# Attention inside a hybrid decoder layer: the scores of a group of heads in one burst, its outputs in one block, its transposes two stages later

## The chip, the cores and the metric

The kernel runs on one core of a Trainium2 chip. The metric is the device time of one execution in microseconds (us); lower is better. Three runs of the kernel before took 1525.62, 1527.35 and 1528.2 us, a median of 1527.35 us.

## What is computed

One decoder layer in float32: 256 tokens, model width 2048. After a norm and one wide input projection, a recurrent branch and an attention branch run side by side, are gated, added and projected, and an MLP of width 8192 follows. The change is in the attention branch alone. It has 32 query heads and 4 key heads of 64 elements; eight query heads share one key head, and these eight are called a group here. Attention goes by blocks of 128 tokens. A query block sees its own block and the one before it, within a window of 128, and each head has a learned sink that takes part in the softmax:

```python
scores = jnp.einsum('bnqhgd,bnkhd->bnhgqk', qb, kk).astype(jnp.float32)   # qb is scaled
scores = jnp.where(valid, scores, NEG_INF)
m = jnp.maximum(jnp.max(scores, axis=-1, keepdims=True), sink)
p = jnp.exp(scores - m)
denom = jnp.sum(p, axis=-1, keepdims=True) + jnp.exp(sink - m)
out = jnp.einsum('bnhgqk,bnkhd->bnqhgd', (p / denom).astype(v.dtype), vv)
```

With 256 tokens there are two query blocks: `tb` 0 sees 128 keys, `tb` 1 sees 256.

## The kernel before

**The stream.** All weights pass through one stream (class `Stream`). SyncE loads halves of 128x1024 float32 (`wraw`, four buffers), ScalarE rounds each to a high part (`whi`, line 94), VectorE subtracts to get the low part (`wlo`, line 95). There are six buffers each of `whi` and `wlo`, and the parts are made six halves ahead, so the cast of half j+6 waits for TensorE to have finished half j. TensorE multiplies each half three ways (high by high, low by high, high by low). In `b_pass512` a half is 12 matmuls of 512 columns (lines 271, 273, 275; outputs `g` and `q`); in `a_pair` it is 8 matmuls of 512 and 8 of 256 columns (lines 253 and 256; output `ps`). Eight halves make one pass. For every group of heads one `g` pass (gates) and one `q` pass (queries) follow each other.

**The attention of a group** is the generator `attention(g, banks)`. It is created after the `q` pass of its group and put on the list `waiting`. The passes that follow call `pump()`, which runs the first generator of the list up to its next `yield`: the `g` pass of the next group pumps after each half, its `q` pass after every second half, `a_pair` after each half. Groups 0, 1 and 2 are so laid into the `g` and `q` passes of groups 1, 2 and 3, and group 3 into the first `a_pair` passes of the recurrent branch. The pumping sets where a step is recorded. A scheduler then orders the instructions of each engine within what the data allow, except for those that `pin` (`tc.keep_in_program_order`) holds in the order of the program. Each engine then works off its instructions strictly in that order.

**Steps of one group.** (1) Rope on the queries, four transposes each for two token blocks into `pq` (line 518), a copy to `qT`. (2) Scores: for a head pair, the two heads lie on partitions 0 to 63 and 64 to 127 of `qT`, so each score matmul uses 64 rows of the array; the two of a pair go to two PSUM banks `sc` (line 540). (3) VectorE scales and masks each bank into `s` (line 547) and takes the row maxima (line 549), three small operations (lines 553 to 555) fold in the sink, ScalarE takes one exponential per head with its row sum (line 560; the sink's is line 556), VectorE adds, inverts (lines 562, 563) and multiplies (line 565). (4) Transposes of the probabilities: four heads of 128x128 into a bank `pt` (line 574), ScalarE copies it to `s` or `pT` (line 576). (5) Outputs: 64-column matmuls with the values `v_sb` into `po` (line 582), the two heads of a pair on the two halves of the columns; ScalarE and VectorE split `po` into `yatt` (lines 586, 587).

For `tb` 0 these are 8 score matmuls of 128 columns, 8 transposes and 2 output matmuls of 512 columns; for `tb` 1, 8 score matmuls of 256 columns, 16 transposes and 4 output matmuls. The profile counts each float32 score and output matmul twice (two passes), each transpose once. Before, `tb` 0 goes through steps 2 to 5 and then `tb` 1 does. All of `pq`, `sc`, `pt` and `po` come from one pool of two PSUM banks (`psm`); another pool of two (`psb`) holds the outputs of the `q` pass, and two pairs of banks (`psa`, handed out by `pair`) hold the outputs of the `g` and `a_pair` passes.

Of the kernel before, what the change touches and what calls it, by code (L numbers as in the profile page):

```python
# [18 lines left out]
F32 = mybir.dt.float32  # L19
# [147 lines left out]
def layer(tc, x, g_pre, pos_t, pos_row, inv_freq, vecs, sinks, gains, w_kv, w_q, w_xy, w_rg, w_g, w_rp, w_ap, w_out,  # L167
# [341 lines left out]
    def attention(g, banks):  # L509
# [11 lines left out]
        for tb in range(TB):  # L521
            yield
            nk = 1 + tb
            w = P * nk
            per = 512 // w
            room = flat(unit("s", F32)).rearrange("p (n c) -> p n c", c=512)
            if tb:
                room_p = flat(unit("pT", F32)).rearrange("p (n c) -> p n c", c=512)
            else:
                room_p = room[:, 2:4, :]  # L530
            stat = pa.tile([P, 4, 8], F32, tag="stat", bufs=3, name="stat")
            sk = sink[:, 8 * g : 8 * g + 8]
            tiles = []
            for j in range(4 // per):
                both = [bank(psm, "sc") for par in range(2)]
                for i in range(per):
                    h = j * per + i
                    for par in range(2):
                        r0 = par * HD
                        mm(both[par][:, i * w : i * w + w], qT[r0 : r0 + HD, h, tb * P : tb * P + P],  # L540
                           kT[r0 : r0 + HD, g, 0:w], start=True, stop=True)
                for par in range(2):
                    ps = both[par]
                    at = par * 4 + j * per
                    s3 = room[:, at // per, :].rearrange("p (h k) -> p h k", h=per)
                    mk = (mask1 if tb else mask0).unsqueeze(1).to_broadcast([P, per, w])
                    nc.vector.scalar_tensor_tensor(s3, ps.rearrange("p (h k) -> p h k", h=per), HD ** -0.5, mk,
                                                   ALU.mult, ALU.add)
                    nc.vector.tensor_reduce(stat[:, 0, at : at + per], s3, AX.X, ALU.max)
                    tiles.append((s3, at))  # L550
                if tb:
                    yield
# [4 lines left out]
            for s3, at in tiles:  # L557
                for i in range(per):
                    c = slice(at + i, at + i + 1)
                    nc.scalar.activation(s3[:, i, :], s3[:, i, :], AF.Exp, bias=stat[:, 1, c],  # L560
                                         accum_out=stat[:, 3, c])
            nc.vector.tensor_tensor(stat[:, 2, :], stat[:, 2, :], stat[:, 3, :], ALU.add)
            nc.vector.reciprocal(stat[:, 2, :], stat[:, 2, :])
            for s3, at in tiles:
                nc.vector.tensor_tensor(s3, s3, stat[:, 2, at : at + per].unsqueeze(2).to_broadcast([P, per, w]),
                                        ALU.mult)
            yield
            pT = {}
            for par in range(2):
                for kb in range(nk):  # L570
                    ps = bank(psm, "pt")
                    for h in range(4):
                        s3, at = tiles[h // per * 2 + par]
                        nc.tensor.transpose(ps[:, h * P : h * P + P], s3[:, h % per, kb * P : kb * P + P], ident)
                    t = room_p[:, par * nk + kb, :]
                    nc.scalar.copy(t, ps)
                    pT[par, kb] = t
            yield
            po = bank(psm, "po")
            for kb in range(nk):  # L580
                for par in range(2):
                    mm(po[par * HD : par * HD + HD, :], v_sb[:, kb, g * HD : g * HD + HD], pT[par, kb],
                       start=kb == 0, stop=kb == nk - 1)
# [676 lines left out]
```

## Time and profile before

| | |
|---|---|
| runs | 1525.62, 1527.35, 1528.2 us (median 1527.35) |
| profiled execution, its own time | 1523.52 us |
| span of its instructions | 1521.7 us |
| mean granted TensorE clock | 0.999 of full |
| TensorE (PE) busy | 1506.0 us, 99% of the span |
| VectorE (DVE) busy | 1105.1 us, 73% |
| ScalarE (ACT) busy | 831.3 us, 55% |

All times in the text are us from the start of the span. In a timeline a row gives the start, the length, the engine, the line and operation, the tiles (written, then read), the shape, how many instructions were merged in it, and in brackets the idle time of the engine ahead of it with what ended it. Matmuls are pipelined: the start of one to the start of the next is what one costs, and the lengths overlap.

### The profile page before, as it was taken

How to read it: one execution, taken by the hardware profiler on the slowest of the kernel's cores; microseconds unless marked ns; L12 is line 12 of the kernel's file. 1: busy time of each engine (PE TensorE's matmuls, PEld its weight loads, DVE VectorE, ACT ScalarE, POOL GpSimd, SP SyncE). 2: the span in 40 equal slices, each digit the busy share in tenths (PEclk: the TensorE clock that was granted, in tenths of full speed). 3: DMA queues.
4: the chain of work that ended last, by engine and by line, in shares of the span. 5: the costliest groups of instructions: out<-in, count | busy, mean ns of one | idle time of the engine just before them, and what ended most of it. 6: DMA issues, size and time to landing. Idle time of an engine off the chain costs nothing.

```text
span 1521.7 us, 20058 instructions
## 1 busy us (share of the span) xinstructions
PE 1506.0 (99%) x7600; PEld 1263.7 (83%) x7600; DVE 1105.1 (73%) x1377; ACT 831.3 (55%) x1143; POOL 5.5 (0%) x11
## 2 busy tenths in 40 slices
PE   9999999999999999999999999999999999999997
PEld 7877778788888888888888888888888888888886
DVE  6666666857759867555667866688886766788897
ACT  6545645746556757444355655555444555555553
POOL 0000000000000000000000000000000000000001
PEclk9999999999999999999999999999999999999999
DMA  6645445354655565555764755556667655566665
GB/s 252 221 153 166 138 142 168 128 188 161 215 184 189 169 219 177 197 195 191 263 225 131 274 198 189 187 182 216 213 202 237 205 187 192 188 230 200 216 221 178
DMA packets 82896, 296.20 MB, mean 195 GB/s; under 512 B 9712, under 2 KB 9968, under 8 KB 81648
## 3 DMA queue, kind: packets, MB, share of 16 engines
q1 hardware_dynamic: 79056, 284.43, 56.4%
q10 hardware_dynamic: 3744, 10.50, 1.9%
q8 instruction: 59, 0.97, 0.3%
q14 instruction: 37, 0.30, 0.1%
HBM read 288.60 MB, written 6.29 MB: 194 GB/s over the span
## 4 chain that ended last, share of the span: by engine, by line
PE 90%; DVE 4%; ACT 2%; DMA 2%; issue 2%; SPq 0%; DVEq 0%; ACTq 0%
PE ps L253 21%; PE ps L256 11%; PE dQ L1036 8%; PE s L1036 4%; PE pp L273 4%; PE pp L275 4%; PE pp L271 4%; PE dP L1036 4%; PE g L271 4%; PE g L275 4%; PE g L273 4%; PE dCs L1036 3%; PE q L271 2%; PE q L273 2%; PE q L275 2%
## 5 line engine op out<-in xcount | busy, mean ns | idle before, releaser
L95 DVE TENSOR_TENSOR wlo<-wraw,whi 128x1024 fp32r<-128x1024 f32 x523 | 634.4, 1222 | 306.2 <-ACT whi L94 304.6
L94 ACT CAST whi<-wraw 128x1024 fp32r<-128x1024 f32 x523 | 544.3, 1051 | 567.4 <-PE ps L253 139.2
L253 PE MATMUL ps<-h2T,whi 128*128 128x512 f32 x960 | 240.5, 393 | 0.0
L253 PEld LDWEIGHTS ps<-h2T,whi 128*128 128x128 f32 x960 | 172.9, 189 | 30.7
L256 PEld LDWEIGHTS ps<-h2T,wlo 128*128 128x128 f32 x960 | 131.0, 191 | 9.3
L256 PE MATMUL ps<-h2T,wlo 128*128 128x256 f32 x960 | 133.9, 283 | 0.0
L253 PE MATMUL ps<-hT,whi 128*128 128x512 f32 x512 | 130.0, 394 | 0.0
L1036 PE MATMUL dQ<-whi,uT 128*128 128x512 f32 x288 | 107.0, 389 | 0.0
L253 PEld LDWEIGHTS ps<-hT,whi 128*128 128x128 f32 x512 | 91.8, 189 | 16.8 <-issue 0.7
L271 PE MATMUL g<-whi,hT 128*128 128x512 f32 x256 | 101.7, 397 | 0.0
L273 PE MATMUL g<-wlo,hT 128*128 128x512 f32 x256 | 100.4, 392 | 0.1
L275 PE MATMUL g<-whi,hT 128*128 128x512 f32 x256 | 100.2, 391 | 0.0
L256 PEld LDWEIGHTS ps<-hT,wlo 128*128 128x128 f32 x512 | 69.8, 191 | 6.3 <-issue 1.5
L256 PE MATMUL ps<-hT,wlo 128*128 128x256 f32 x512 | 71.9, 283 | 0.0
L1036 PEld LDWEIGHTS dQ<-whi,uT 128*128 128x128 f32 x288 | 54.1, 188 | 11.2
L271 PEld LDWEIGHTS g<-whi,hT 128*128 128x128 f32 x256 | 48.1, 188 | 10.9 <-issue 1.3
L275 PEld LDWEIGHTS g<-whi,hT 128*128 128x128 f32 x256 | 48.1, 188 | 10.6 <-issue 0.7
L273 PEld LDWEIGHTS g<-wlo,hT 128*128 128x128 f32 x256 | 48.2, 188 | 9.7 <-DVE wlo L95 0.5
L1036 PE MATMUL dQ<-wlo,uT 128*128 128x512 f32 x144 | 56.1, 389 | 0.0
L130 DVE TENSOR_TENSOR tlo<-t,thi 128x1536 fp32r<-128x1536 f32 x28 | 49.2, 1757 | 6.8 <-ACT thi L129 6.8
L1036 PE MATMUL dP<-whi,uT 128*128 128x512 f32 x144 | 54.1, 389 | 0.0
L1036 PE MATMUL dCs<-whi,uT 128*128 128x512 f32 x144 | 54.1, 389 | 0.0
(280 smaller groups left out, 2477.4 us busy)
## 6 DMA issues: line engine op xcount, KB each, us to landing
wraw<-in_w_up SPq DMA_DIRECT2D x128, 512.0 KB, 4.7
wraw<-in_w_dn SPq DMA_DIRECT2D x128, 512.0 KB, 4.6
wraw<-in_w_g SPq DMA_DIRECT2D x64, 512.0 KB, 4.8
wraw<-in_w_xy SPq DMA_DIRECT2D x64, 512.0 KB, 4.6
wraw<-in_w_q SPq DMA_DIRECT2D x32, 512.0 KB, 3.7
wraw<-in_w_ap SPq DMA_DIRECT2D x32, 512.0 KB, 4.7
wraw<-in_w_rp SPq DMA_DIRECT2D x32, 512.0 KB, 4.4
wraw<-in_w_out SPq DMA_DIRECT2D x32, 512.0 KB, 5.2
```

The source lines that it names most:

```text
L94: self.pin(self.nc.scalar.copy(hi, src))
L95: self.pin(self.nc.vector.tensor_tensor(lo, src, hi.bitcast(F32), ALU.subtract))
L130: v.tensor_tensor(lo, t, hi.bitcast(F32), ALU.subtract)
L253: mm(both, hi[:, k * P : k * P + P], a.rearrange("p a b -> p (a b)"), start=half == 0 and k == 0, stop=False)
L256: mm(ps[:, f, 1, :], lo[:, k * P : k * P + P], a[:, 0, :], start=False, stop=half == 1 and k == 7)
L271: mm(banks[tb][n], a[:, 0, t], hi[:, n * 512 : n * 512 + 512], start=first, stop=False)
L273: mm(banks[tb][n], a[:, 0, t], lo[:, n * 512 : n * 512 + 512], start=False, stop=False)
L275: mm(banks[tb][n], a[:, 1, t], hi[:, n * 512 : n * 512 + 512], start=False, stop=last)
L1036: mm(b, a[x], w[y], start=not begun and i == 0, stop=tail and i == 2)
```

## The change

The generator is cut in functions, and the order of its steps changes:

- **Scores.** Both token blocks are computed at one place, at the third `yield`: the banks of `tb` 0 from `psm`, half of those of `tb` 1 from `psb`, and the other half from a pair of `psa`, so that six banks are in use. The matmuls are pinned in program order, which alternates the two heads of a pair. In the last group the second half of `tb` 1 comes one stage later, from `psb` again.
- **Softmax** of `tb` 0 follows at once, that of `tb` 1 a stage later.
- **Transposes** of `tb` 0 two stages after the scores, those of `tb` 1 two stages after that.
- **Outputs** of both blocks at the end, pinned.

No operation is added or removed: there are the same matmuls, transposes, copies and vector operations.

```diff
-        for tb in range(TB):
-            yield
-            nk = 1 + tb
...
-            for j in range(4 // per):
-                both = [bank(psm, "sc") for par in range(2)]
...
-                        mm(both[par][:, i * w : i * w + w], qT[r0 : r0 + HD, h, tb * P : tb * P + P],
-                           kT[r0 : r0 + HD, g, 0:w], start=True, stop=True)
...
-                if tb:
-                    yield
+        def scores(tb, j, both):
...
+            for i in range(per):
+                h = j * per + i
                 for par in range(2):
+                    r0 = par * HD
+                    pin(mm(both[par][:, i * w : i * w + w], qT[r0 : r0 + HD, h, tb * P : tb * P + P],
+                           kT[r0 : r0 + HD, g, 0:w], start=True, stop=True))
+            for par in range(2):
...
+                nc.vector.scalar_tensor_tensor(s3, both[par].rearrange("p (h k) -> p h k", h=per), HD ** -0.5, mk,
+                                               ALU.mult, ALU.add)
+                nc.vector.tensor_reduce(stats[tb][:, 0, at : at + per], s3, AX.X, ALU.max)
...
+        def softmax(tb):
...
+        def turn_probs(tb):
...
+        last_group = g == NKV - 1
+        scores(0, 0, [bank(psm, "sc") for par in range(2)])
+        scores(1, 0, [bank(psb, "sc") for par in range(2)])
+        if not last_group:
+            scores(1, 1, two_banks("sc"))
+        softmax(0)
+        yield
+        if last_group:
+            scores(1, 1, [bank(psb, "sc") for par in range(2)])
+        softmax(1)
+        yield
+        turn_probs(0)
+        yield
+        yield
+        turn_probs(1)
+        yield
+        for tb in range(TB):
             po = bank(psm, "po")
-            for kb in range(nk):
+            for kb in range(1 + tb):
                 for par in range(2):
-                    mm(po[par * HD : par * HD + HD, :], v_sb[:, kb, g * HD : g * HD + HD], pT[par, kb],
-                       start=kb == 0, stop=kb == nk - 1)
+                    pin(mm(po[par * HD : par * HD + HD, :], v_sb[:, kb, g * HD : g * HD + HD], pT[tb, par, kb],
+                           start=kb == 0, stop=kb == tb))
```

The functions hold the lines that stood in the loop, in the same order within each.

The order of instructions shows what the scheduler makes of it. First TensorE in group 1, around the end of the `g` pass, as it stands before. `pt` are the transposes, `po` the outputs, `sc` the scores, `s` the probabilities; `g` and `q` are matmuls of the stream.

```order
L574 MATMUL pt<-ident,s 128x128 x8
L273 MATMUL g<-wlo_1306,hT_136 128x512
L275 MATMUL g<-whi_1305,hT_136 128x512
L582 MATMUL po<-s,v_sb 64x512 x2
L540 MATMUL sc<-kT,qT_1266 128x256 x2
L271 MATMUL g<-whi_1305,hT_136 128x512
L273 MATMUL g<-wlo_1306,hT_136 128x512
L275 MATMUL g<-whi_1305,hT_136 128x512
L540 MATMUL sc<-kT,qT_1266 128x256 x2
```

The scores of `tb` 1 stand in three places (a block of four follows), two of them with both matmuls of one bank next to each other, and the outputs of `tb` 0 stand alone. With the change, the same group has its scores together some 50 rows earlier, and its outputs together at the end:

```order
L275 MATMUL g<-whi_1209,hT_134 128x512
L537 MATMUL sc<-kT,qT_1265 128x128 x8
L537 MATMUL sc<-kT,qT_1265 128x256 x8
L271 MATMUL g<-whi_1227,hT_135 128x512
...
L271 MATMUL q_1529<-whi_1329,hT_133 128x512
L581 MATMUL pt<-ident,s 128x128 x8
L273 MATMUL q_1529<-wlo_1330,hT_133 128x512
...
L271 MATMUL q_1529<-whi_1436,hT_134 128x512
L607 MATMUL po<-s,v_sb 64x512 x2
L607 MATMUL po<-pT,v_sb 64x512 x4
L273 MATMUL q_1529<-wlo_1437,hT_134 128x512
```

Between the last score and the first transpose stand 49 matmuls of the stream in groups 1 and 2 and 55 in group 0; between that and the outputs stand 24, with the sixteen transposes of `tb` 1 in three places among them.

Second, VectorE in the same group, from the scores to the first normalised probabilities, before:

```order
L547 SCALAR_TENSOR_TENSOR s<-sc,mask_422 128x512 x2
L549 TENSOR_REDUCE stat<-s 128x4 x2
L553 TENSOR_TENSOR stat<-stat,sink 128x8
L554 TENSOR_SCALAR stat<-stat 128x8
L555 TENSOR_TENSOR stat<-sink,stat 128x8
L95 TENSOR_TENSOR wlo_1411<-wraw_1278,whi_1410 128x1024
L562 TENSOR_TENSOR stat<-stat 128x8
L563 RECIPROCAL stat<-stat 128x8
L565 TENSOR_TENSOR s<-s,stat 128x512 x2
```

and with the change:

```order
L543 SCALAR_TENSOR_TENSOR s<-sc,mask_422 128x512 x2
L545 TENSOR_REDUCE stat<-s 128x4 x2
L543 SCALAR_TENSOR_TENSOR s<-sc,mask_422 128x512 x2
L545 TENSOR_REDUCE stat<-s 128x2 x2
...
L552 TENSOR_TENSOR stat<-stat,sink 128x8
L95 TENSOR_TENSOR wlo_1437<-wraw_1277,whi_1436 128x1024
L553 TENSOR_SCALAR stat<-stat 128x8
L552 TENSOR_TENSOR stat<-stat,sink 128x8
L554 TENSOR_TENSOR stat<-sink,stat 128x8
...
L564 TENSOR_TENSOR s<-s,stat 128x512 x2
```

All six banks are masked and reduced (the left-out pair repeats the two lines above it) and one `wlo` is made before the maxima of `tb` 0 reach ScalarE.

Third, ScalarE in the last group with the change, between the exponentials of `tb` 1 and the split of the outputs:

```order
L94 CAST whi87_2566<-wraw87_2429 128x1024
L583 COPY pT_2469<-pt_2470 128x512
L583 COPY pT_2469<-pt_2476 128x512
L94 CAST whi88_2588<-wraw88_2451 128x1024
L583 COPY pT_2469<-pt_2482 128x512
L583 COPY pT_2469<-pt_2488 128x512
```

The cast of half 88 stands ahead of the last two copies; it needs the buffer of half 82, whose last matmuls stand on TensorE just ahead of the outputs of this group. Before, all four copies stood together. After the last group the order of all engines is as before, and the loads on SyncE stand in the same order throughout.

54 lines of the change are left out of this document (26 added, 28 removed).

## The prediction

> **What bounds the kernel now.** I read the page first: the share of each engine, and the chain of work that ended last.
>
> ```profile
> PE 1506.0 (99%) x7600; PEld 1263.7 (83%) x7600; DVE 1105.1 (73%) x1377; ACT 831.3 (55%) x1143; POOL 5.5 (0%) x11
> PE 90%; DVE 4%; ACT 2%; DMA 2%; issue 2%; SPq 0%; DVEq 0%; ACTq 0%
> ```
>
> TensorE is busy 99% of the span and carries 90% of the chain. No weight transfer and no other engine sets the pace, so the change is worth what it alters in TensorE's own sequence: the time that score, transpose and output matmuls take there, and the time that TensorE stands still for their operands. Reordering work on VectorE or ScalarE counts only through the second.
>
> Next, the busy time in four stretches, each from the first score matmul of a group to the return to the stream after its last output (for the last group, to the next start of a weight half). The columns are the stretch, its length, TensorE's busy time and count, its granted clock, and two on DMA.
>
> ```profile
> 92.80:132.00 39.20, 39.09 (x189) 1.00 0.43 140
> 149.55:188.70 39.15, 38.79 (x189) 1.00 0.42 141
> 206.25:245.40 39.15, 38.79 (x189) 1.00 0.43 142
> 263.13:304.01 40.88, 40.52 (x230) 1.00 0.39 129
> ```
>
> Then the timeline of TensorE in group 1, for the price of each piece.
>
> ```profile
> 149.55 1.16 PE L540 MATMUL sc<-kT,qT 64*128 64x128 f32 x16
> 150.64 0.50 PE L271 MATMUL g<-whi,hT 128*128 128x512 f32 x1
> ...
> 162.50 1.13 PE L540 MATMUL sc<-kT,qT 64*128 64x256 f32 x4
> 163.55 0.50 PE L271 MATMUL g<-whi,hT 128*128 128x512 f32 x1
> ...
> 167.09 1.14 PE L540 MATMUL sc<-kT,qT 64*128 64x256 f32 x8
> 168.16 0.50 PE L271 MATMUL q<-whi,hT 128*128 128x512 f32 x1
> 168.49 0.39 PE L273 MATMUL q<-wlo,hT 128*128 128x512 f32 x1
> ...
> 179.18 1.03 PE L574 MATMUL pt<-ident,s 128*128 128x128 f32 x8
> 179.97 0.48 PE L271 MATMUL q<-whi,hT 128*128 128x512 f32 x1
> 180.29 0.40 PE L273 MATMUL q<-wlo,hT 128*128 128x512 f32 x1
> ...
> 181.74 0.60 PE L574 MATMUL pt<-ident,s 128*128 128x128 f32 x4
> 182.09 0.48 PE L273 MATMUL q<-wlo,hT 128*128 128x512 f32 x1
> 182.41 0.39 PE L275 MATMUL q<-whi,hT 128*128 128x512 f32 x1
> ...
> 186.52 0.39 PE L275 MATMUL q<-whi,hT 128*128 128x512 f32 x1
> 186.83 1.94 PE L582 MATMUL po<-pT,v_sb 128*64 128x512 f32 x8
> 188.70 0.50 PE L271 MATMUL q<-whi,hT 128*128 128x512 f32 x1
> ```
>
> From 182.41 to 186.52 there are 18 steps of the stream: 0.228 us each. Group 1 holds 68 attention instructions (32 of scores, 24 transposes, 12 of outputs) and 120 of the stream, one more lying across the edge. So its attention costs TensorE 39.15 - 120 x 0.228 = 11.8 us now, and groups 0 and 2 the same.
>
> The rows to see next are the two score rows of 256 columns: four instructions (two matmuls) from 162.50 to 163.55 take 1.05 us, and eight (four matmuls) from 167.09 to 168.16 take 1.07. In the first both use the same 64 rows of the array; in the second the two heads alternate and run side by side. The change pins the alternation everywhere.
>
> **The change, part by part.** Leaving the stream for 64-row scores or 64-column outputs costs 0.31 instead of 0.228 ahead (186.52 to 186.83), and 0.33 instead of 0.228 behind (168.16 to 168.49): about 0.2 a visit. Transposes cost 0.09 on return alone (179.97 to 180.29).
>
> *Scores, groups 0 to 2.* One block instead of four: 1.09 + 2 x 1.06 = 3.2, less two joints of 0.2, is 2.8, and 0.1 on return. Its bounds are 2.8 and 3.2; I take 2.8, since nothing leaves the 64-row form in between.
>
> *Transposes.* Those of `tb` 0 stay one block of 0.79, with return 0.88. Those of `tb` 1 stand as 4, 4 and 8: 2 x 0.35 + 0.79 + 3 x 0.09 = 1.76.
>
> *Outputs.* One block of twelve instructions instead of four and eight. Eight take 1.87; half of that without the 0.2 is 0.83, so 2.7, and 0.08 on entry: 2.8.
>
> Without any wait a group then costs 2.9 + 0.88 + 1.76 + 2.8 = 8.3 us, 3.5 below now.
>
> *The wait that the change adds* stands before the first transposes, because VectorE now clears six banks before `tb` 0's softmax goes on. The rows of group 1 now, VectorE, then ScalarE, then TensorE:
>
> ```profile
> 151.87 1.28 DVE L547 SCALAR_TENSOR_TENSOR s<-sc,mask 128x512 f32<-128x512 f32 x2
> 153.07 1.27 DVE L549 TENSOR_REDUCE stat<-s 128x4 f32<-128x512 f32 x2
> ...
> 158.31 0.17 DVE L562 TENSOR_TENSOR stat<-stat 128x8 f32<-128x8 f32 x1 [2.22 <-ACT s L560]
> 158.51 0.20 DVE L563 RECIPROCAL stat<-stat 128x8 f32<-128x8 f32 x1
> 158.75 0.69 DVE L565 TENSOR_TENSOR s<-s,stat 128x512 f32<-128x512 f32 x1
> ```
>
> ```profile
> 154.99 0.21 ACT L556 ACTIVATE stat<-stat 128x8 f32<-128x8 f32 x1 [0.23 <-DVE stat L555]
> ```
>
> ```profile
> 159.59 1.23 PE L574 MATMUL pt<-ident,s 128*128 128x128 f32 x8 [0.26 <-DVE s L565]
> ```
>
> Two banks take 1.2 for the mask and 1.2 for the maxima (151.87 to 153.07). Six end at 151.87 + 3 x 2.4 = 159.1. From the end of the maxima to ScalarE it is 0.65 now (153.07 + 1.27 = 154.34, to 154.99). With one `wlo` between (1.2, filling some 0.25 of gaps) it is 1.6: 160.7. Exponentials up to the sum's use take 3.32 (154.99 to 158.31): 164.0. Sum and inverse 0.44, the first product 0.69, then 0.15 to TensorE (159.44 to 159.59): 165.3. TensorE arrives after the burst and 49 stream matmuls, at 149.55 + 2.9 + 49 x 0.228 = 163.6. So it waits 1.7, and 0.2 more for the second product (0.6 behind the first, with 0.4 of transposes between): 1.9 in groups 1 and 2. In group 0 six more matmuls, 1.4 us, stand between: 0.5. Behind the waiting transposes the whole stream is queued, so nothing hides this. The bounds are nothing and, if TensorE had to stand until VectorE has cleared the burst (7.2 us for 2.8 of scores), 4.4 a group. I take the value from the rows, because the 49 matmuls of the stream need none of the six banks.
>
> On this the Trainium skill has a rule that speaks against the change. TensorEngine Tiling (Array Packing), section PSUM Bottleneck, says that tiling speeds up TensorE and not the emptying of PSUM, which can become the bottleneck, and that ScalarE and VectorE should both empty it; here VectorE does it alone. Were the emptying the bottleneck, as that section has it, the sum would be the slower rival's below. The trace agrees as far as the 0.26 of waiting at 159.59 goes, with two banks to empty.
>
> *Smaller waits.* `tb` 1's exponentials now run straight behind `tb` 0's on ScalarE, and its products are ready about when TensorE has done the 13 matmuls that follow. The last transposes and outputs need banks of `psm` that ScalarE copies out, with one cast between the pairs of copies. I estimate 0.4 a group, between 0 and the 1.05 of one cast (row below).
>
> Group 0 costs 8.3 + 0.5 + 0.4 = 9.2, a gain of 2.6. Groups 1 and 2 cost 8.3 + 1.9 + 0.4 = 10.6, a gain of 1.2 each.
>
> *The last group* lies in `a_pair`. The length of its weight halves, and the price of a cast and of a copy:
>
> ```profile
> 285.93 2.00 PE L253 MATMUL ps<-hT,whi 128*128 128x512 f32 x8
> ...
> 297.10 0.62 PE L253 MATMUL ps<-hT,whi 128*128 128x512 f32 x2
> ```
>
> ```profile
> L94 ACT CAST whi<-wraw 128x1024 fp32r<-128x1024 f32 x523 | 544.3, 1051 | 567.4 <-PE ps L253 139.2
> ```
>
> ```profile
> 160.25 0.58 ACT L576 COPY s<-pt 128x512 f32<-128x512 f32 x1
> ```
>
> Four halves from 285.93 to 297.10 are 2.79 each. The stretch holds ten, so attention costs 40.88 - 27.9 = 13.0 now. With the change: 12 score matmuls in one block 2.05, four in a second 1.25, transposes 2.64, outputs 2.8, in all 8.7. The waits are larger. The second block reuses `psb` banks that VectorE reaches late, about 0.8. The first transposes wait about 1.1, by the chain above with VectorE's convolution steps in it; the first of `tb` 1 about 0.8. The outputs wait for the last copies, which stand on ScalarE behind the cast of half 88; that cast starts only when TensorE has finished half 82, one stream matmul before the outputs: 1.05 + 0.58 + 0.1 - 0.23 = 1.5. Sum 8.7 + 4.2 = 12.9: no gain, between -2 and +4.
>
> *The stream's own supply.* Halves 36 and later get their `wlo` up to 9 us later than now, because VectorE and ScalarE do the softmax of both blocks first. The six halves made ahead cover 6 x 12 x 0.228 = 16 us, so I count nothing; without that cover each us late would be a us.
>
> Sum: 2.6 + 1.2 + 1.2 + 0 = 5.0 us less. The profiled execution takes 1523.52, 3.8 below the median of the runs; it would come to 1518.5, and the median from 1527.35 to 1522.4.
>
> **Rivals.** *The waits vanish* (the chain is shorter, or TensorE arrives later): 3.5 in three groups and 13.0 - 8.7 in the last, 14.8 less: 1512.6. Against it stands that TensorE waits for line 565 already now, with only two banks ahead of it. Chance 0.08.
>
> *The gain is eaten on ScalarE.* If one cast (1.05) stands in the way of one copy in every group, that is 4 x 1.05 = 4.2, and 1526.6 is left. For it speaks the last group's order; against it that the casts between the copies in groups 0 to 2 need halves long finished. Chance 0.20.
>
> *Slower: VectorE's clearing of the burst is the bound.* Place: between the last score and the first transposes of groups 0 to 2. If TensorE stands there for the upper bound, 4.4 in each instead of 0.5, 1.9 and 1.9, that is 8.9 more than counted, 3.9 more than now: 1531.3. It decides from 1.7 us a group on, where 3 x 1.7 eats the 5.0. For it speaks that VectorE has work without a break from 151.87 on. Against it stands the order, which has 49 to 55 stream matmuls, 11 to 12.5 us, in between. Chance 0.07.
>
> *Slower by the clock.* TensorE, left idle, could come back at a lower clock. If it ran at half clock for as long as each wait, 1.9 us, that would cost some 1 to 2 us a group. That is 4 to 8 in all, so between 1526.4 and 1530.4; the granted clock is 1.00 in all four stretches, waits of 0.26 included. Chance 0.03. TensorE: Matmul & The Clock Gate, section Part 1, in the Trainium skill, has the clock halved after an idle window of about 3.4 us; by that rule the waits counted here are too short to trigger it. No run here shows an idle time of that length.
>
> **How the numbers follow.** The forecast has 0.62: a gain of 3 to 8, so 1519.5 to 1524.3. About 0.2% (3 us) is what a measurement can tell here. Faster is the forecast with the first rival: 0.70; within 0.2% the second: 0.20; slower the last two: 0.10. The range leaves out the first rival below and the two slower ones above: 1517.5 to 1527.5, which allows for the spread of the runs, 1.3 either side.
>
> **What would show it.** Right: the scores of groups 0 to 2 stand as one row pair of about 2.8 us, eight instructions of 256 columns in half the time per matmul; the first transposes carry a bracket of 1.5 to 2 us from line 564 in groups 1 and 2 and a small one in group 0; stretches of equal stream work shorten by 2.6, 1.2, 1.2 and 0; the outputs of the last group wait for ScalarE. Wrong: stream matmuls that wait for `wlo`, a bracket before the first transposes above 3 us, or a burst longer than 3.2.

## The result

The changed kernel takes 1518.56 us (median of 5 runs, 1517.1 to 1520.64) where the kernel before takes 1527.35 (5 runs, 1525.62 to 1528.2): a ratio of 0.9945, 95% interval 0.9933 to 0.9956. It is faster by 8.8 us. The forecast was 1522.4 with a range of 1517.5 to 1527.5, so the sign and the range hold and the gain is 3.8 us larger than said. Of these, 1.9 us lie in the last group and 1.3 in the other three, as the groups below show; the remaining 0.5 is the difference between the groups and the medians.

The page of the changed kernel, its busy times and the shares of the chain that ended last:

```profile
PE 1496.4 (99%) x7600; PEld 1259.9 (83%) x7600; DVE 1103.0 (73%) x1377; ACT 828.7 (55%) x1143; POOL 5.5 (0%) x11
PE 82%; DVE 9%; DMA 5%; ACT 2%; issue 2%; DVEq 0%; SPq 0%; ACTq 0%
```

TensorE has the same 7600 instructions as before and is busy 9.6 us less. VectorE now has 9% of the chain instead of 4%. Next, the four stretches, from a group's first score matmul to the return to the stream behind its last output (stretch, length, TensorE's busy time and count, granted clock, DMA share, GB/s):

```profile
93.31:120.24 26.93, 26.86 (x149) 1.00 0.34 106
147.04:173.92 26.88, 25.45 (x143) 1.00 0.34 108
202.08:228.95 26.87, 25.45 (x143) 1.00 0.35 106
257.31:296.80 39.49, 38.59 (x232) 1.00 0.42 135
```

The stretches hold less of the stream than before, because scores and outputs are now closer together: 79, 73 and 73 stream matmuls by the program's order, instead of 120 in each of groups 0 to 2. At 0.228 us each, attention costs 26.93 - 18.0 = 8.9 us in group 0 and 26.88 - 16.6 = 10.2 in groups 1 and 2, instead of 11.8. In groups 1 and 2 TensorE is idle for 1.43 of it. The granted clock is 1.00 throughout.

What a group gained is read best from one stream matmul that both programs have. In the trace of before, then of the changed kernel, the first matmul of the gate pass ahead of group 0's attention and the first of the attention projection behind the last group:

```profile
80.87 0.39 PE L271 MATMUL g<-whi,hT 128*128 128x512 f32 x1
309.60 0.40 PE L271 MATMUL pp<-whi,yatt 128*128 128x512 f32 x1
```

```profile
81.40 0.39 PE L271 MATMUL g<-whi,hT 128*128 128x512 f32 x1
301.84 0.40 PE L271 MATMUL pp<-whi,yatt 128*128 128x512 f32 x1
```

From one to the other it is 228.73 us before and 220.44 now: the four groups give 8.29 us. Taken in the same way at the first matmul of each next gate or recurrence pass, they give 3.04, 1.66, 1.65 and 1.94. That is the whole difference of the medians, 8.8, within the spread of the runs. (The two profiled spans, 1521.7 and 1516.8, differ by 4.9 only: the profiled execution of before was 3.8 below its median. Another profiled execution of the changed kernel, x6 below, has a span of 1512.4 and the same 8.30 in the groups.)

TensorE's timeline of group 1 answers to the one in the prediction. The columns are start, length, engine, line, operation, tiles, shape; the bracket is the idle time ahead and what ended it.

```profile
147.04 2.89 PE L537 MATMUL sc<-kT,qT 64*128 64x128 f32 x32
162.73 1.23 PE L581 MATMUL pt<-ident,s 128*128 128x128 f32 x8 [1.43 <-DVE s L564]
...
171.19 1.08 PE L607 MATMUL po<-s,v_sb 128*64 128x512 f32 x4
172.10 1.89 PE L607 MATMUL po<-pT,v_sb 128*64 128x512 f32 x8
173.92 0.50 PE L273 MATMUL q<-wlo,hT 128*128 128x512 f32 x1
```

The burst of 32 instructions is one row of 2.89 us, where the scores stood in four places. The outputs take 173.92 - 171.19 = 2.73. Between them stands the added wait, for VectorE's product of line 564. VectorE's rows for that wait, then ScalarE's:

```profile
149.36 1.28 DVE L543 SCALAR_TENSOR_TENSOR s<-sc,mask 128x512 f32<-128x512 f32 x2
...
155.32 1.27 DVE L545 TENSOR_REDUCE stat<-s 128x2 f32<-128x512 f32 x2
156.51 0.16 DVE L552 TENSOR_TENSOR stat<-stat,sink 128x8 f32<-128x8 f32 x1
156.58 1.22 DVE L95 TENSOR_TENSOR wlo<-wraw,whi 128x1024 fp32r<-128x1024 f32 x1
...
161.45 0.17 DVE L561 TENSOR_TENSOR stat<-stat 128x8 f32<-128x8 f32 x1 [1.94 <-ACT s L559]
...
161.89 1.29 DVE L564 TENSOR_TENSOR s<-s,stat 128x512 f32<-128x512 f32 x2
```

```profile
158.12 0.21 ACT L555 ACTIVATE stat<-stat 128x8 f32<-128x8 f32 x1 [1.40 <-DVE stat L554]
```

Six banks are cleared from 149.36 to 156.51 (7.2 us), a split of weights stands in the middle of the small steps at 156.58 as forecast, the exponentials take from 158.12 to 161.45 (3.33), and the first product lets TensorE go at 162.73, 15.7 us behind the start of the burst: the forecast's 165.3 - 149.55 = 15.75.

### The profile page after: what moved, and what is told of

Its sections match the earlier page's. It is cut to its first block, busy times and chain, and to the rows that moved or that the text cites. A ratio compares the mean times of both kernels' runs of the same rounds, so it can differ in the third digit from the quotient of the medians.

```text
span 1516.8 us, 20055 instructions
## 1 busy us (share of the span) xinstructions
PE 1496.4 (99%) x7600; PEld 1259.9 (83%) x7600; DVE 1103.0 (73%) x1377; ACT 828.7 (55%) x1143; POOL 5.5 (0%) x11
## 4 chain that ended last, share of the span: by engine, by line
PE 82%; DVE 9%; DMA 5%; ACT 2%; issue 2%; DVEq 0%; SPq 0%; ACTq 0%
PE ps L253 22%; PE ps L256 11%; PE dQ L1061 4%; DMA wraw<-in_w_dn 4%; PE pp L271 4%; PE pp L275 4%; PE pp L273 4%; PE g L271 3%; PE g L275 3%; PE g L273 3%; DVE wlo L95 3%; PE s L1061 2%; PE dP L1061 2%; PE q L273 2%; PE q L275 2%; PE q L271 2%
```

## The experiments

**The theory.** TensorE is the bound, so the gain is what leaves its sequence (visits to the 64-row and 64-column forms, and score matmuls that did not run side by side) less what it now stands still for VectorE's softmax chain. **Rivals:** the gain is the joining alone, whichever rows are used; the waits are a cost of going over to transposes and no chain; part of the difference is run to run; a wait taken away comes back elsewhere. The table has what each run gave. "Groups" is the time from the one stream matmul to the other, less than before; the difference of the medians is against the kernel before in the same runs.

| run | groups 0, 1, 2, last | sum | medians, less by | ratio, 95% interval |
|---|---|---|---|---|
| the change | 3.04, 1.66, 1.65, 1.94 | 8.3 | 8.8 | 0.9945 (0.9933 to 0.9956) |
| x1 rows one behind the other in a block | 1.54, 1.03, 1.02, 2.13 | 5.7 | 5.6 | 0.9959 (0.9943 to 0.9974) |
| x2 transposes three stages later | 2.24, 1.16, 2.14, 1.97 | 7.5 | 5.9 | 0.9955 (0.9939 to 0.9970) |
| x3 softmax first | 1.50, -0.28, 1.31, 1.87 | 4.4 | 3.7 | 0.9972 (0.9962 to 0.9983) |
| x4 softmax first, two stages later | 0.33, -1.00, 1.84, 2.28 | 3.5 | 4.8 | 0.9969 (0.9956 to 0.9982) |
| x5 softmax first, spaced | 1.55, 1.32, 1.30, 1.89 | 6.1 | 5.1 | 0.9961 (0.9948 to 0.9974) |
| x6 the change again | 3.04, 1.67, 1.65, 1.94 | 8.3 | 9.4 | 0.9933 (0.9919 to 0.9947) |
| x7 upper rows first | 1.53, 0.99, 1.01, 1.96 | 5.5 | one execution | |
| x8 outputs apart | 2.61, 1.23, 1.23, 1.92 | 7.0 | one execution | |
| x9 spaced, copies first | 2.60, 0.49, -1.21, 1.90 | 3.8 | 4.7 | 0.9967 (0.9954 to 0.9980) |
| x10 later, copies first | 2.24, 1.85, 1.83, 1.97 | 7.9 | one execution | |
| x11 four banks | 2.90, 3.48, 3.48, 1.87 | 11.7 | 11.8 | 0.9928 (0.9916 to 0.9941) |
| x12 four banks, later | 3.55, 3.48, 3.48, 1.82 | 12.3 | 12.4 | 0.9923 (0.9909 to 0.9936) |

The groups are read from one execution of each kernel; x7, x8 and x10 were executed only once, so they have no median of their own. In the runs that were repeated the groups alone give the difference of the medians within 1.6 us.

### x6: the change again

The same kernel, in the runs of x5.

> The changed kernel as it is, once more, in the same runs as the others. Theory: the four groups gain 8.3 us and nothing else differs, so the difference of the medians is 8 to 9 us, ratio 0.994 to 0.995, with first waits of 0.2, 1.6, 1.6 and 0.9 us again. Rival (part of the difference was run to run): a ratio of 0.996 or more.

The groups gave the same to 0.01 us, and the medians 9.4. The gain is no accident of the runs, and it lies in the four groups. Waits that hang on transfers from memory do not repeat so well, as x10 shows below.

### x1 and x7: which rows stand side by side

x1 turns the two loops of a block's score matmuls:

```diff
-            for i in range(per):
-                h = j * per + i
-                for par in range(2):
+            for par in range(2):
+                for i in range(per):
+                    h = j * per + i
                     r0 = par * HD
```

> The changed kernel, but the score matmuls of a block run first through all heads of the upper 64 rows and then through those of the lower 64, instead of alternating. Theory: part of the gain is the alternation, since two heads on different rows run side by side; without it the burst of 32 instructions takes some 4.9 us instead of 2.8, about 2.1 more in each of groups 0 to 2 and as much in the last, so the time is 8 us or more above the changed kernel's 1518.6: about 1527, no gain left. The transposes also stand a little differently (40 stream matmuls behind the burst instead of 49 in groups 1 and 2, in two pieces), which adds or takes less than 1 us. Rival (the gain is the joining of the blocks, whichever rows they use): the burst stays at 2.8 to 3.2 us and the time within 2 us of 1518.6.

The burst took 3.37 us, not 4.9: the expectation failed, and so did its arithmetic, which took every matmul of x1 to stand alone. x7 puts all of the upper rows of all three blocks first:

```diff
+        def products(blocks):
+            for par in range(2):
+                r0 = par * HD
+                for tb, j, both in blocks:
...
+                    for i in range(per):
+                        pin(mm(both[par][:, i * w : i * w + w], qT[r0 : r0 + HD, j * per + i, tb * P : tb * P + P],
+                               kT[r0 : r0 + HD, g, 0:w], start=True, stop=True))
```

> The changed kernel, but the burst runs through all sixteen half-matmuls of the upper 64 rows, of all three blocks, and then through those of the lower 64. The run that put the rows one behind the other inside each block lengthened the burst by 0.55 us only, not by 2.1. Theory: matmuls on different rows run side by side only with their neighbours in the queue, and in that run the neighbours at each change of rows still overlapped; with one change of rows in the burst almost nothing overlaps, and it takes 4.6 to 5 us. Rival (the rows matter little, the price is in the visits): 3.4 us again.

The burst of x1, of x7, and the return to the stream behind each:

```profile
148.99 3.44 PE L537 MATMUL sc<-kT,qT 64*128 64x128 f32 x32
152.36 0.50 PE L271 MATMUL g<-whi,hT 128*128 128x512 f32 x1
```

```profile
148.19 4.75 PE L533 MATMUL sc<-kT,qT 64*128 64x128 f32 x32
152.87 0.50 PE L271 MATMUL g<-whi,hT 128*128 128x512 f32 x1
```

2.82 us alternating, 3.37 in x1, 4.68 in x7, for the same 32 instructions. The expectation of x7 had the time right and the reason too narrow: it is not the nearest neighbour alone that runs alongside. In x7's trace the first lower-row instruction starts at 150.05, beside the upper rows' 256-column instruction at 150.05, while three more upper ones, at 150.26, 150.48 and 150.69, are still to come; the lower rows go on beside them. So the second half of the rows starts when the first has four instructions (two matmuls) left. At each change of rows x1 shows the same, or a start that comes later because those rows were still busy. One half of the rows takes 8 x 0.111 + 8 x 0.216 = 2.62 us. With that rule the three orders take 2.62, 3.06 and 4.37 us; measured are 0.20, 0.31 and 0.31 more, which is the entry, the return and, in x1 and x7, a first lower-row instruction that takes 0.1 longer. The rule is read from these orders and was not tried on another.

The alternation is worth something, but x1's groups also lose by their transposes: 40 stream matmuls behind the burst (46 in group 0), they wait 1.8 us in groups 1 and 2 and 1.4 in group 0. The rival with the visits alone is out, by x7; how much of the change's gain the pins themselves bring was not tried apart.

### x8: the outputs in two places

```diff
         turn_probs(1)
-        yield
         for tb in range(TB):
+            yield
             po = bank(psm, "po")
```

> The changed kernel with the outputs of the first block at one stage and those of the second at the next, as before, with everything else on TensorE in the same place. Theory: a visit to the 64-column form costs 0.2 to 0.3 us, so the two blocks together take 0.2 to 0.3 us more per group than the 2.73 + 0.33 of the one, and the whole comes to 1 us more than the changed kernel. Rival (the outputs were not shortened by being joined): no difference.

Rows of x8's group 1, outputs and return:

```profile
172.30 1.08 PE L607 MATMUL po<-s,v_sb 128*64 128x512 f32 x4
173.31 0.50 PE L273 MATMUL q<-wlo,hT 128*128 128x512 f32 x1
...
178.76 1.94 PE L607 MATMUL po<-pT,v_sb 128*64 128x512 f32 x8
180.62 0.50 PE L271 MATMUL q<-whi,hT 128*128 128x512 f32 x1
```

1.01 and 1.86 are 2.87 instead of 2.73, and a second entry and return stand around them; the groups 0 to 2 gained 0.43 less each (in the last group the order of the two did not come apart). Joining the outputs is worth 0.4 a group, somewhat more than the 0.2 to 0.3 expected.

### x2: the transposes later

```diff
         softmax(1)
         yield
+        yield
+        yield
+        yield
         turn_probs(0)
```

> The changed kernel with the first transposes issued three stages later: 72 stream matmuls stand between the burst and the first transposes in groups 0 to 2 instead of 55, 49 and 49, and 64 instead of 33 in the last group. Theory: the 1.6 us that the first transposes wait in groups 1 and 2, the 0.2 in group 0 and the 0.9 in the last are VectorE's and ScalarE's softmax chain, which ends some 16 to 17 us after the burst's start; TensorE now comes 19.3 us after it, so all four waits go, 4.3 us in all: about 1514.3. Rival 1 (the bracket is a cost of going over to the transposes, whenever they come): the waits stay and the time is that of the changed kernel, 1518.6. Rival 2 (buffers that are held longer starve the stream, or the next group's query transposes come behind late work): new waits on the stream matmuls, 1518 or more.

At the first transposes TensorE waits nowhere any more, so rival 1 is out: the wait was the chain. But the gain fell to 7.5. TensorE now stands at the second transposes, at their third bank (TensorE, then ScalarE, in group 1):

```profile
182.82 0.66 PE L581 MATMUL pt<-ident,s 128*128 128x128 f32 x4 [2.04 <-ACT pT L583]
```

```profile
179.97 1.05 ACT L94 CAST whi<-wraw 128x1024 fp32r<-128x1024 f32 x1 [2.04 <-DMA wraw<-in_w_g]
181.23 1.05 ACT L94 CAST whi<-wraw 128x1024 fp32r<-128x1024 f32 x1 [0.21 <-DMA wraw<-in_w_g]
182.19 1.06 ACT L583 COPY pT<-pt 128x512 f32<-128x512 f32 x2
```

The four transposed blocks share two banks. The third needs the first one's copy, and that stands on ScalarE behind two casts, the first of which waits 2.04 us for weights from memory. This is the prediction's rival of the gain eaten on ScalarE, brought up by moving the transposes. The weights are late because SyncE issued no load in group 1 between 160.4 and 170.5: it waits for buffers that VectorE frees with the splits of line 95, and VectorE, busy with the softmax, starts none between 159.17 and 169.22. The changed kernel has such a gap too (159.5 to 169.6), but its copies are through at 171.4, before the first of the late loads lands at 173.4. One cast stands between the pairs of copies there, and started without a gap:

```profile
165.36 1.05 ACT L583 COPY s<-pt 128x512 f32<-128x512 f32 x2
166.31 1.05 ACT L94 CAST whi<-wraw 128x1024 fp32r<-128x1024 f32 x1
```

### x3, x4 and x5: the softmax of the first block ahead of the other clearing

x3 parts the clearing from the matmuls and puts the first softmax between:

```diff
+        clear(0, 0, b0)
+        softmax(0)
+        clear(1, 0, b1)
...
+            clear(1, 1, b2)
-        softmax(0)
         yield
```

> The changed kernel with VectorE's work in another order: it clears the two banks of the first block, goes on to that block's small softmax steps and only then clears the four banks of the second (two or three of their steps still stand between). The transposes move up as well: 26 stream matmuls behind the burst in groups 1 and 2 instead of 49, 31 instead of 55 in group 0, 20 instead of 33 in the last. Theory (TensorE waits where its arrival is before the end of the chain, one for one): the chain now ends about 12.2 us after the burst's start, by 4.7 for the first two banks, 2.6 for the steps between, 3.6 for ScalarE and 1.3 for sum, inverse and product; TensorE arrives at 2.9 + 26 x 0.228 = 8.8, so it waits 3.4 in groups 1 and 2 instead of 1.6, some 2.2 in group 0 instead of 0.2, and 1 more in the last: about 1525. Rival (what counts is the clearing of all six banks, so to start the softmax earlier takes the waits away): 1514 to 1516.

TensorE waits at the first transposes in each group again: by brackets 1.92 in groups 1 and 2, less than the 3.4 expected (the chain lets it go 11.0 us behind the burst's start at 148.89, not 12.2), but more than the 1.43 of the change. The rival is out. The chain did get shorter, and the transposes moved up by more. Group 1, however, lost 1.6 us more than group 2 with the same wait. Its row, then two windows around this wait and two around the same wait in group 2 (the column after the count in brackets is the granted clock):

```profile
159.86 0.63 PE L586 MATMUL pt<-ident,s 128*128 128x128 f32 x4 [1.92 <-DVE s L569]
```

```profile
157.80:161.21 3.41, 1.49 (x11) 1.00 0.00 0
161.21:164.62 3.41, 3.41 (x9) 0.50 0.45 149
212.41:215.82 3.41, 2.52 (x12) 1.00 0.00 0
215.82:219.24 3.42, 2.39 (x15) 1.00 0.01 2
```

For 3.41 us TensorE runs at a granted clock of 0.50 and starts a stream matmul every 0.427 us. That is the prediction's rival of the clock, which the changed kernel does not show. Why the one wait brings it and the other does not is worked out in the last section.

x4 issues the transposes two stages later than x3 (two more `yield` ahead of `turn_probs(0)`).

> The same order on VectorE as in the run before, with the transposes issued two stages later, so that 48 stream matmuls stand between the burst and the first transposes in every group. Theory: the chain ends about 12.2 us after the burst's start and TensorE arrives at 2.9 + 48 x 0.228 = 13.8, so no group waits at its first transposes: 4.3 us below the changed kernel, about 1514.3, and 11 below the run before, although TensorE does the same work. Rival (the order on VectorE decides, not the distance): as the run before, within 2 us.

The first waits are gone, as the theory had it, but the time is not 11 us below x3: it is the same within the intervals, which the rival predicted for another reason. As in x2 the wait has moved to the second transposes, by brackets 2.92, 2.58 and 1.35 us in groups 0 to 2, behind ScalarE's copies, and in group 1 the clock falls again:

```profile
179.50 0.66 PE L586 MATMUL pt<-ident,s 128*128 128x128 f32 x4 [2.58 <-ACT pT L588]
```

```profile
180.27:183.68 3.41, 3.41 (x12) 0.50 0.72 256
```

x5 puts the first transposes 36 stream matmuls behind the burst and leaves the second ones where x3 has them:

```diff
         softmax(1)
         yield
+        yield
         turn_probs(0)
         yield
-        yield
         turn_probs(1)
```

> The order on VectorE of the run with the softmax first, and the stages of the transposes set by what the runs so far measured: the first transposes one stage later than there (36 stream matmuls behind the burst in groups 0 to 2), the second ones where they stood there, 12 to 14 matmuls behind the first and spread out, where no wait was seen. Theory: in the run with the softmax first TensorE waited 2.1 us at 26 matmuls (2.31 from the matmul before it, less the usual 0.23), so the chain ends 9 matmuls later and 36 are enough; the second transposes keep their banks, since ScalarE's copies stand where they stood. All waits in groups 0 to 2 go: 5.7 us less than in that run, 3 less than in the changed kernel, so a ratio of about 0.992 to 0.993, beside the changed kernel's own in the same runs. Rival (the wait always comes back at the second transposes, which need ScalarE's copies, as in the two runs with later transposes): 1 to 2 us at the second transposes of each group, and no better than the changed kernel.

The rival held. Group 1:

```profile
159.87 1.04 PE L586 MATMUL pt<-ident,s 128*128 128x128 f32 x8
164.64 0.44 PE L586 MATMUL pt<-ident,s 128*128 128x128 f32 x2 [0.98 <-ACT s L588]
165.60 0.87 PE L586 MATMUL pt<-ident,s 128*128 128x128 f32 x6 [0.52 <-DVE s L569]
```

No wait at 159.87, and 1.5 us at the second transposes: by the brackets 0.98 for a bank that ScalarE copies out late and 0.52 for VectorE's product. The expectation forgot that a TensorE that is not held at the first transposes comes to the second that much sooner: the copies and the second block's chain end when they end.

### x9 and x10: ScalarE's copies ahead of its casts

x9 has the second transposes 72 stream matmuls behind the burst, where VectorE has long finished, and both runs ask for the copies ahead of other work:

```diff
+                    with tc.high_priority(200):
-                    nc.scalar.copy(t, ps)
+                        nc.scalar.copy(t, ps)
```

> The order on VectorE of the run with the softmax first; the first transposes 36 stream matmuls behind the burst in groups 0 to 2, where the spaced run had no wait in groups 1 and 2; the second ones 72 behind instead of 48, since in the spaced run TensorE, no longer held at the first, came to the second 1.9 us before VectorE's products; and ScalarE's copies out of the banks of the transposes go ahead of casts wherever the order allows it (one or two casts instead of five stand ahead of the second pair of copies). Theory (a wait ends only where both the chain and ScalarE's copies are done before TensorE arrives): no wait at the first transposes of groups 1 and 2, 0.4 in group 0, none for products at the second, and up to 1 us for a copy behind a cast in each group; the four groups gain 9 to 12 us instead of 8.3, 1514 to 1518, ratio 0.991 to 0.995. Rival (the cast in front of a copy waits for its weights, and the copy with it, as in the run with the transposes later): 1.5 to 3 us at the second transposes of each group, a gain of the groups of 4 to 7 us, ratio 0.996 or more.

> The run with the transposes three stages later, with nothing changed but the order on ScalarE: the copies out of the banks of the transposes go ahead of casts wherever the order allows it. There TensorE waited 1.3 to 2.2 us at the second transposes of each group behind copies that stood behind casts. Theory (the casts in front of the copies are the cause): those waits shrink by half or more, and the four groups gain 9.5 to 12 us by the end of the last group instead of 7.5. Rival (the two banks are the cause, one copy after the other): the same waits, the same 7.5.

In x9 both the chain and the first transposes are clear in groups 1 and 2, and still the rival came: 2.69 and 2.8 us at the third bank, and a slow clock behind the second of these. ScalarE in group 1:

```profile
170.63 1.04 ACT L94 CAST whi<-wraw 128x1024 fp32r<-128x1024 f32 x1 [3.17 <-DMA wraw<-in_w_q]
171.58 1.07 ACT L589 COPY pT<-pt 128x512 f32<-128x512 f32 x2
```

The cast ahead of the copies waits 3.17 us for its weights while the banks are full. x10 tells little of its question: in groups 0 to 2 the request moved the copies of the second transposes past no cast, so what was to be changed was not, and the waits stayed, 1.3 to 1.5 us from the matmul ahead. It tells something else: in groups 1 and 2 the order on TensorE, VectorE and ScalarE is that of x2, and yet the gains are 1.85 and 1.83 instead of 1.16 and 2.14. Waits that hang on transfers differed here by up to 0.7 us a group between two executions.

### x11 and x12: four banks

The second transposes take the pair of banks that the last score block has left, besides the two small ones; all four blocks are transposed ahead of the first copy.

```diff
+            four = tb and not last_group
+            if four:
+                pool = pairs[-1]
+                more = pool.tile([P, 2, 2, S], F32, tag="pair" + pool.name, name="pt")
...
-                    ps = bank(psm, "pt")
+                    ps = more[:, kb].rearrange("p a b -> p (a b)") if par and four else bank(psm, "pt")
```

> The stages of the spaced run with the copies first (first transposes 36 stream matmuls behind the burst, second ones 72), but the second transposes of groups 0 to 2 get four banks instead of two: the pair that the last score block has just left besides the two small ones. They stand as one block of 16 instructions and wait for no copy of ScalarE's; the outputs stand 24 stream matmuls behind them. Theory (what held the two runs with late transposes was the third bank, free only after a copy that stands behind a cast which waits for its weights): the waits of 2.8 us at the second transposes go, with only 0.4 in group 0 left at the first and up to 1 us at the outputs where the copies are late; attention costs 8.6 to 9.2 us a group instead of 12.1 before, the last group gains 1.9 as ever, and the four groups gain 10.5 to 12.5 us: 1514.5 to 1517 against 1527, ratio 0.991 to 0.993. Rival (the wait moves on to the outputs, which need all copies): 2 us or more in front of the outputs of each group, a gain of 4 to 7 us, ratio 0.996 or more.

> As the run with four banks, with the first transposes one stage later still (48 stream matmuls behind the burst; the second ones stay at 72, the outputs at 96). Theory: the 0.4 us at the first transposes of group 0 goes too, and nothing else changes in groups 0 to 2; in the last group the 0.9 us in front of its second transposes shrinks and its outputs stand in two pieces, 0.3 more: within 1 us of the run with four banks, ratio 0.990 to 0.993. Rival: as there, the copies come late for the outputs, ratio 0.996 or more.

x12's stretches of groups 0 to 2:

```profile
93.04:123.30 30.26, 30.26 (x166) 1.00 0.39 133
146.26:176.52 30.26, 30.26 (x166) 1.00 0.42 143
199.48:229.74 30.26, 30.26 (x166) 1.00 0.45 146
```

TensorE is busy 30.26 of 30.26 us in each of the three, with 96 stream matmuls in it: attention costs 30.26 - 96 x 0.228 = 8.4 us, with no wait left. That is the prediction's 8.3 for a group without waits, measured, though with the second transposes in one block instead of three. Both runs did as the theory said (11.7 and 12.3 in the groups, 11.8 and 12.4 in the medians), but for one detail of x12: the wait in the last group's second transposes did not shrink (brackets of 0.81 us, and 0.82 in x11). Both beat the kernel before and the change: ratios 0.9928 and 0.9923, against 0.9945 and 0.9933 for the change in its two measurements. The intervals overlap those of the change in both its measurements, most where the change did best (0.9909 to 0.9936 for x12, 0.9919 to 0.9947). That x12 beats the change rests on the groups, which leave 4.0 us between the two: the change's repeat to 0.01 us, and x12's groups 0 to 2 have no wait that could vary.

## Why the prediction was right, and where it was not

- **The burst.** Forecast 2.8, and 0.1 on return: 149.86 - 147.04 = 2.82 by the row behind it, and 0.11 (0.34 to the next start, less 0.228). Right. The reason, alternation, is right too; x1 and x7 add how far ahead the other rows can start.

```profile
149.86 0.51 PE L271 MATMUL g<-whi,hT 128*128 128x512 f32 x1
```

- **Transposes and outputs.** 2.73 for the outputs, with 0.1 on entry: the 2.8. With no wait at all the whole came to 8.4 (x12) for a forecast of 8.3.
- **The added wait** in groups 0 to 2. Forecast 0.5, 1.9 and 1.9, with 0.2 of these for the second product. From the matmul ahead TensorE lost 0.2, 1.6 and 1.6, and 0.2 more inside the block in each. Right in place, releaser and size; the chain's 15.7 us were met to 0.1. x2, x3 and x12 bear out that the wait is the chain's end less TensorE's arrival: it goes where TensorE comes later (x2, x12) and grows where TensorE comes earlier by more than the chain was shortened (x3).
- **Smaller waits.** Forecast 0.4 a group, measured under 0.1: the later transposes start as soon as the matmul ahead of them lets them. The one cast between ScalarE's copies did not make them late. This is why groups 0 to 2 gave 3.04, 1.66 and 1.65 instead of 2.6, 1.2 and 1.2. The bound was set right (nothing to one cast), the value at the wrong end of it. x2, x4 and x9 show what the other end looks like: 1.5 to 2.9 us, since the cast not only takes its 1.05 but waits for its weights.
- **The stream's own supply.** Forecast nothing, and in the four groups of the changed kernel no stream matmul waits for its weights. Right for the stream; but the same delay of loads and splits came back in x2, x4 and x9 through the casts ahead of the copies, a path that the prediction did not follow.
- **The last group.** Forecast no gain, measured 1.94. The step that failed is the outputs' 1.5 us behind the cast of half 88, "that cast starts only when TensorE has finished half 82". TensorE in the changed kernel, with half 82's low matmuls and the next half's first, then ScalarE:

```profile
283.09 0.40 PE L256 MATMUL ps<-hT,wlo 128*128 128x256 f32 x2
283.32 1.07 PE L581 MATMUL pt<-ident,s 128*128 128x128 f32 x8
284.15 0.96 PE L256 MATMUL ps<-hT,wlo 128*128 128x256 f32 x6
284.94 0.39 PE L253 MATMUL ps<-hT,whi 128*128 128x512 f32 x1
285.27 1.08 PE L607 MATMUL po<-s,v_sb 128*64 128x512 f32 x4
```

```profile
282.61 1.08 ACT L583 COPY pT<-pt 128x512 f32<-128x512 f32 x2
283.57 1.06 ACT L94 CAST whi<-wraw 128x1024 fp32r<-128x1024 f32 x1
284.52 1.08 ACT L583 COPY pT<-pt 128x512 f32<-128x512 f32 x2
```

  The cast of half 88 starts at 283.57, straight behind the copies and 1.4 us ahead of the end of half 82. It writes `whi`, which is a buffer of its own; the last reader of half 82's is a high matmul that stands ahead of the row at 283.09, and the low matmuls read `wlo`. The copies end at 285.60. The outputs of `tb` 0, from 285.27, need none of them, and those of `tb` 1 follow 0.91 us later, at 286.18: neither waited. The term was too large in a second way, since the prediction let all outputs wait for the last copies, though the 0.91 us of `tb` 0 stand ahead of those that need them. The other waits of the last group were 0.8 at the second score block (forecast 0.8), 1.15 at the first transposes (1.1), 0.2 at the second (0.8). So two terms were too large, by 1.5 and 0.6 us, which gives the 1.94 within 0.2.
- **The rivals.** None of them decided the change. Two showed in the experiments, at other places: the copy behind a cast (x2, x4, x5, x9) and the clock (x3, x4, x9). The slower one, with VectorE's clearing as the bound, did not: x2 clears the six banks in the same order and has no wait at the first transposes, and x12 clears six banks and has no wait at all in groups 0 to 2.

## What to carry to other kernels

When an engine that is the bound waits, shortening or moving past that wait gives the next one its turn: work out where the bound engine arrives everywhere behind it, with the wait gone, and when each operand and each bank is ready there. In an in-order queue a short copy is as late as the slowest operand of the work ahead of it, so look at what that work waits for, and not only at how long it takes; a spare pair of banks took away here what none of the reorderings tried did. Read the release of a buffer from its own readers, high and low halves apart.

## What was not expected of the hardware

- A wait of TensorE's of 1.9 us can cost more than itself, and the traces show when. In each trace the changes of the clock lie whole multiples of 3.41 us apart (in x3 the slow stretches begin at 7.61 and at 161.21, which is 45 x 3.413), and within the kernel a slow stretch at 0.50 lasts one such window. In all fourteen traces TensorE's idle time within one window tells the clock of the next. The seven waits of 1.9 us or more at the transposes, the largest other one, and two for comparison:

| run and group | wait, us | idle in the fuller window, us | clock of the next window |
|---|---|---|---|
| x9, group 2 | 2.81 | 2.81 | 0.50 |
| x4, group 1 | 2.58 | 2.58 | 0.50 |
| x3, group 1 | 1.92 | 1.92 | 0.50 |
| x4, group 0 | 2.92 | 1.74 | 1.00 |
| x1, group 2 | 1.68 | 1.68 | 1.00 |
| x2, group 1 | 2.04 | 1.65 | 1.00 |
| x9, group 1 | 2.69 | 1.57 | 1.00 |
| the change, group 1 | 1.43 | 1.43 | 1.00 |
| x3, group 2 | 1.92 | 1.02 | 1.00 |
| before, start of the kernel | 1.55 | 1.55 | 1.00 |

  At the start of the kernel, six more windows with 1.94 to 2.09 us of idle time (x1, x3, x5, x8, x10, x11) were each followed by one at 0.50. So the bound lies between 1.74 and 1.92 us of idle time in a window of 3.41: the longest wait, 2.92 us, cost no clock, because it fell across two windows. A slow window costs half of 3.41, 1.7 us; x3's group 1 lost 1.6 against its twin. Where a longer wait falls in the windows differs from one execution to the next, so the sums of x3, x4 and x9 in the table hold one such loss each by chance; the 1.43 us of the changed kernel are below the bound wherever they fall. In the Trainium skill, TensorE: Matmul & The Clock Gate, section Part 1, has a free-running window of about 3.4 us, after an idle one of which the clock is halved; the traces agree on the window, its length and the halving, and they differ in that a window with 1.92 us of idle time was enough.
- Score matmuls on different 64 rows ran side by side beyond their nearest neighbours in the queue, but not far: the other rows started when four instructions were left of the run ahead, so three orders of the same 32 instructions took 2.82, 3.37 and 4.68 us.
